# Sixteen gate products, placed between the parts of the recurrence batches instead of behind the last batch

## The chip, the cores and the metric

The kernel runs on one core of a Trainium2 chip. The metric is the device time of the program in microseconds (us). Three runs of the kernel before took 3376.48, 3397.38 and 3405.18 us; the median is 3397.38 us. One further execution was profiled.

## The reference, cut to what matters

The program computes two transformer-like blocks. The change lies in the first one, in its token mixer, where a Hyena branch and an RWKV-7 branch are joined by gates:

```python
def token_mixer(h, p, states0):
    cols = h @ p['w_in']
    hy_cols, rw_cols, gate_cols = jnp.split(cols, (HY_COLS, HY_COLS + RW_COLS), axis=-1)
    y_hy = hyena_branch(hy_cols, p) @ p['hy_proj']
    y_rw, finals = rwkv_branch(rw_cols, p, states0)
    g_hy, g_rw = jnp.split(jax.nn.sigmoid(gate_cols), 2, axis=-1)
    mixed = (g_hy * y_hy + g_rw * (y_rw @ p['rw_proj'])) @ p['w_out']
    return mixed, finals
```

There are 512 tokens of width 1024, and 256 context tokens that only give start states. The RWKV recurrence `S <- S (diag(w) + a^T b) + v^T k` runs over the tokens for 8 heads of 64 and in both directions. The gates need `h` and `w_in` alone: they depend on no recurrence, and nothing in the recurrences depends on them.

## The kernel before, in words

**The recurrences.** `rwkv` (line 627) cuts them into six batches. Batches 0 and 1 are the context, batches 2 to 5 the 512 tokens, one pair of heads in both directions each. Time is cut into chunks of 64, inside which the recurrence becomes matrix products and one triangular inverse. A batch has these parts:

- `rw_start`: the products of h with w_in for k, v and r (`win_mm`, 24 matmuls of 128x512 each, tiles `mm<-hTh,wh`), the norm of k (lines 723, 732, 738; its end is `kk`, L769), the low-rank products (L797), then a run of DVE, ACT and POOL steps (L799 to L833) that ends with `kms` (L840).
- `rw_gram`: products of one chunk with itself (L863), in four pieces, masked on ACT and DVE.
- `rw_inverse`: DVE alone. L891 transposes, then 31 pairs of L899 and L900, the substitution row by row.
- `rw_blocks`: L910 and L911 on DVE, then two sets of 32x32 products (L920, L928), copied by ACT (L923, L931).
- `rw_rows` and `rw_ops`: transposes and products (L953 to L993, then L1020, L1033).
- `rw_chain`: the states in order, each step two small matmuls (L1063) and one DVE operation (L1068), and then the output `py` (L1081, L1084), copied out by ACT (L1086).
- `rw_end`: the group norm of the output (L704 to L715); that of the last batch ends with L712.

In the loop (line 662) the start and gram of batch i+1 are written ahead of the inverse, blocks, rows and chain of batch i. The tile `AR` has two buffers, so the start of batch i+2 cannot finish writing it before the `py` of batch i has read it.

**The gates.** `fill` (line 548) makes 16 gates, one for each 128 columns: eight of kind `wgh`, eight of kind `wgr`. For each, `h_mm` (line 262) loads two halves of the weight (tag `wf`, four buffers that the loaded, the high and the low part share), makes the high part on ACT (L279) and the low part on POOL (L280), and issues 24 matmuls in float32r (L285 to L287, tiles `sm<-hTh,wh`; `sm` has one buffer). ACT takes the tanh (L556), POOL scales it (L557), multiplies it for `wgh` (L561) and writes it to memory (L562). In the code all of it stands behind the last batch.

**What sets the order.** The tile framework orders each engine's instructions when the program is built. The text order is the priority; work that stands later in the text is moved up where the scheduler's own model finds an engine free. So some of the gates stood inside the batches already. On the chip each engine then takes its instructions in that fixed order.

**What follows.** `mix_out` (line 1260) closes the pools of the recurrences, loads the outputs of the batches (L1282), multiplies them by their gate (L1283), and multiplies by `rw_proj` (L1292 for the first three batches, L1300 for the last).

Of the kernel before, what the change touches and what calls it, by code (L numbers as in the profile page):

```python
# [178 lines left out]
class K:  # L179
# [365 lines left out]
            nc.scalar.activation(o, ps, AF.Copy)  # L545
            nc.gpsimd.dma_start(self.mhd[c], o)

    def fill(self, pool):

        nc, I = self.nc, self.I  # L550
        for w_, dst in (("wgh", self.mhd), ("wgr", self.grd)):
            for c in range(KD):
                ps = self.psum("sm", 1)
                self.h_mm(ps, I[w_][c], "wf", self.nwf, nc.gpsimd)
                g = self.rw["wk"].tile([P, T], F32, name="hyo")
                nc.scalar.activation(g, ps, AF.Tanh, scale=0.5)  # L556
                nc.gpsimd.tensor_scalar(g, g, 0.5, 0.5, op0=OP.mult, op1=OP.add)  # L557
                if w_ == "wgh":
                    h = self.rw["wk"].tile([P, T], F32, name="hyi")
                    nc.gpsimd.dma_start(h, self.mhd[c])  # L560
                    nc.gpsimd.tensor_tensor(g, g, h, op=OP.mult)  # L561
                nc.gpsimd.dma_start(dst[c], g)  # L562

    def skip(self, moe):

        xp = self.xp = self.pool(self.top, "xp", side="right")
        self.X = xp.tile([P, TT, D], F32, name="X")
        self.nc.sync.dma_start(self.X, self.I["t_x"])
        with ExitStack() as es:
            z = self.pool(es, "zp").tile([P, 512], F32, name="zz")  # L570
            for t in range(TT if not moe else 0):
                for h in range(2):
                    self.nc.vector.memset(z, 0.0)
                    self.add_to_x(t, h, z)
        self.open_stream(6)
        with ExitStack() as es:
            w1 = self.pool(es, "w1")
            self.silu_vec(w1)
            self.mtag = "tr"
            for g in (1, 2) if moe else ():  # L580
                list(self.lat_group(g, w1))
            list(self.ada_group(0, 0, w1))
            if not moe:
                for g in range(3):
                    list(self.ada_group(1, g, w1))
                list(self.s5_prep(w1))
        if moe:
            self.mes = ExitStack()
            self.rtw = self.pool(self.mes, "yl").tile([P, KD, NEXP], F32, name="rtw")
            self.nc.sync.dma_start(self.rtw, self.I["rtw"])  # L590
            self.open_moe()
            self.route_weights()
            with ExitStack() as es:
                wk = self.pool(es, "mo2", bufs=2)
                for t in range(TT):
                    self.route_logits(t, wk, *self.route_tile(t, wk, wk.tile([P, KD, P], F32, name="h2T"), wk.tile([P, D], F32, name="junk")))
                for t in range(TT):
                    self.first_rows(t)
                self.first_rank(0, wk)
# [27 lines left out]
    def rwkv(self):  # L627


        nc, I = self.nc, self.I  # L630
        V, G = nc.vector, nc.gpsimd
        es = ExitStack()
        self.nwi, self.wit = 4, "wi"
        with es:
            cst = self.pool(es, "rwc")
            wk = self.pool(es, "rwk")
            wupa = cst.tile([P, 2, 512], F32, name="wupa")
            nc.scalar.dma_start(wupa[0:64], I["wup"])
            nc.scalar.dma_start(wupa[64:128], I["aup"])
            mid = cst.tile([P, 14], F32, name="mumid")  # L640
            mu0, mu1 = self.col("rw_mu", 0, 14), self.col("rw_mu", 14, 14)
            V.tensor_tensor(mid, mu0, mu1, op=OP.add)
            V.tensor_scalar(mid, mid, -1.0, 1.0, op0=OP.mult, op1=OP.add)
            h = cst.tile([P, 2, 8], F32, name="halfb")
            V.tensor_scalar(h[:, 0], self.col("rw_w0", 0, 8), 0.5, None, op0=OP.mult)
            V.tensor_scalar(h[:, 1], self.col("rw_a0", 0, 8), 0.5, None, op0=OP.mult)
            ka = cst.tile([P, 2, 4], F32, name="ka")
            V.tensor_scalar(ka[:, 0], self.col("rw_k_a", 0, 4), 0.5, None, op0=OP.mult)
            V.tensor_scalar(ka[:, 1], self.col("rw_k_a", 0, 4), -0.5, 1.0, op0=OP.mult, op1=OP.add)

            S0 = cst.tile([P, 8, CH], F32, name="S0")
            LLc = cst.tile([P, TC], F32, name="LLc")
            LL = cst.tile([P, T], F32, name="LL")
            self.rw = dict(wupa=wupa, halfb=h, ka=ka, S0=S0, wk=wk, mid=mid)
            self.mix(12, self.win_mm(24, True), LLc)
            self.mix(12, self.win_mm(24), LL)
            nc.scalar.activation(LLc[0:64], LLc[0:64], AF.Tanh)
            nc.scalar.activation(LL[0:64], LL[0:64], AF.Tanh)
            B = [dict(cts=(2 * i, 2 * i + 1), n=TC, LL=LLc) for i in range(2)] + [dict(cts=(i,), n=T, LL=LL) for i in range(4)]
            self.rw_start(B[0])  # L660
            self.rw_gram(B[0])
            for i, b in enumerate(B):
                if i + 1 < len(B):
                    self.rw_start(B[i + 1])
                    self.rw_gram(B[i + 1])
                self.rw_inverse(b)
                self.rw_blocks(b)
                self.rw_rows(b)
                self.rw_chain(b)
                if b["out"]:  # L670
                    self.rw_end(b)
                if i == 0:
                    self.hy_out()
                    self.rw_gate()
            self.fill(None)
            self.dump("d_S0", S0)

    def mix(self, i, ps, out):
# [1758 lines left out]
```

## Time and profile before

| | |
|---|---|
| median of three runs | 3397.38 us |
| profiled execution | 3396.03 us, span 3394.3 us |
| PE (TensorE matmul) busy over the span | 92% |
| DVE, ACT, POOL busy | 48%, 28%, 21% |
| mean granted TensorE clock | 0.947 |

The recurrences of the tokens lie between about 404 and 846 us, the rest of the gates between 846 and 896 us. A busy PE in this profile is not PE at its peak: matmuls overlap, and their ends are modelled. "Idle before" is time in which an engine had nothing running, with what ended it. An instruction that fails to find its input holds up all that is behind it on the same engine.

### The profile page before, as it was taken

How to read it: one execution, taken by the hardware profiler on the slowest of the kernel's cores; microseconds unless marked ns; L12 is line 12 of the kernel's file. 1: busy time of each engine (PE TensorE's matmuls, PEld its weight loads, DVE VectorE, ACT ScalarE, POOL GpSimd, SP SyncE). 2: the span in 40 equal slices, each digit the busy share in tenths (PEclk: the TensorE clock that was granted, in tenths of full speed). 3: DMA queues.
4: the chain of work that ended last, by engine and by line, in shares of the span. 5: the costliest groups of instructions: out<-in, count | busy, mean ns of one | idle time of the engine just before them, and what ended most of it. 6: DMA issues, size and time to landing. Idle time of an engine off the chain costs nothing.

```text
span 3394.3 us, 42711 instructions
## 1 busy us (share of the span) xinstructions
PE 3128.7 (92%) x16973; PEld 1973.0 (58%) x16973; DVE 1627.2 (48%) x2862; ACT 942.7 (28%) x1707; POOL 729.3 (21%) x793
## 2 busy tenths in 40 slices
PE   8989989989789999999999988899888998999999
PEld 3646556666465334333333257565776777778887
DVE  3665887663052211110110146775676776546464
ACT  3313443332131111111101032246331332234242
POOL 1031231333320143330000033110596002210000
PEclk9998997869989999999999999789998998999999
DMA  5643210001559999999999954310336465422221
GB/s 217 222 175 106 66 38 29 29 32 57 211 198 356 372 421 420 420 421 421 420 421 421 420 219 160 124 56 13 121 127 220 158 203 153 140 81 97 96 99 69
DMA packets 144591, 681.41 MB, mean 201 GB/s; under 512 B 25455, under 2 KB 33815, under 8 KB 76424
## 3 DMA queue, kind: packets, MB, share of 16 engines
q1 hardware_dynamic: 134480, 652.44, 50.4%
q0 software_dynamic: 5536, 18.16, 1.4%
q10 hardware_dynamic: 4376, 8.09, 0.7%
q8 instruction: 134, 2.20, 0.3%
q14 instruction: 65, 0.53, 0.0%
HBM read 654.50 MB, written 24.12 MB: 200 GB/s over the span
## 4 chain that ended last, share of the span: by engine, by line
PE 56%; DMA 17%; DVE 12%; POOL 8%; issue 4%; ACT 3%; SPq 0%; ACTq 0%; POOLq 0%; DVEq 0%
DMA we<-in_w_dram 13%; PE mm L1635 8%; PE mm L285 5%; PE mm L286 5%; PE mm L287 5%; PE ch L1667 3%; POOL cug L2051 3%; PE sm L287 2%; PE sm L286 2%; PE sm L285 2%; PE tr L1549 2%; DMA wa<-in_adaw_dram 2%; POOL sca L2052 1%; DVE macc L347 1%; PE sm L1598 1%
## 5 line engine op out<-in xcount | busy, mean ns | idle before, releaser
L1635 PE MATMUL mm<-we,XG 128*64 128x512 f32 x2048 | 473.4, 601 | 4.2 <-DMA we<-in_w_dram 3.4
L285 PE MATMUL mm<-hh,wh 128*128 128x512 f32 x704 | 281.3, 400 | 22.8 <-DVE vg L2005 18.5
L1635 PEld LDWEIGHTS mm<-we,XG 128*64 128x64 f32 x2048 | 134.1, 137 | 273.2 <-issue 254.1
L286 PE MATMUL mm<-hl,wh 128*128 128x512 f32 x704 | 277.6, 394 | 0.0
L1667 PE MATMUL ch<-we,hid 128*64 128x512 f32 x1024 | 263.2, 598 | 13.0 <-DMA we<-in_w_dram 12.9
L287 PE MATMUL mm<-hh,wl 128*128 128x512 f32 x704 | 271.8, 394 | 0.0
L1590 DVE SCALAR_TENSOR_TENSOR hth<-hth,tr 128x256 f32<-128x256 f32 x64 | 27.0, 421 | 394.3 <-ACT hth L1589 393.8
L1667 PEld LDWEIGHTS ch<-we,hid 128*64 128x64 f32 x1024 | 94.8, 136 | 170.4 <-issue 132.2
L285 PEld LDWEIGHTS mm<-hh,wh 128*128 128x128 f32 x704 | 134.1, 190 | 65.3 <-issue 25.9
L347 DVE SCALAR_TENSOR_TENSOR macc<-wa,cvs,macc 128x512 f32<-128x512 f32 (+1 forms) x119 | 151.6, 1291 | 34.1 <-DMA wa<-in_adaw_dram 29.5
L470 POOL TENSOR_TENSOR X<-X,gy 128x512 f32<-128x512 f32 x20 | 28.2, 1433 | 591.5 <-DVE gy L1737 591.5
L280 DVE TENSOR_TENSOR wl<-wu,wh 128x1024 fp32r<-128x1024 f32 x88 | 118.1, 1343 | 72.4 <-ACT wh L279 72.1
L287 PEld LDWEIGHTS mm<-hh,wl 128*128 128x128 f32 x704 | 134.0, 190 | 29.3
L286 PEld LDWEIGHTS mm<-hl,wh 128*128 128x128 f32 x704 | 134.4, 191 | 26.9 <-POOL hl L464 0.6
L1603 DVE TENSOR_TENSOR acc<-acc,sm 128x512 f32<-128x512 f32 x48 | 33.0, 687 | 236.4 <-PE sm L1598 236.4
L1646 ACT ACTIVATE hs<-mm 128x512 f32<-128x512 f32 x64 | 38.2, 597 | 386.9 <-PE mm L1635 380.2
L279 ACT ACTIVATE wh<-wu 128x1024 fp32r<-128x1024 f32 x88 | 93.3, 1060 | 132.6 <-PE mm L286 99.9
L280 DVE TENSOR_TENSOR wl<-wd,wh 128x1024 fp32r<-128x1024 f32 (+1 forms) x48 | 56.9, 1187 | 95.4 <-ACT wh L279 95.4
L1720 POOL TENSOR_TENSOR ess<-ess,mhalf 128x1 f32<-128x1 f32 x4 | 3.2, 792 | 442.7 <-DVE ess L1719 442.6
L279 ACT ACTIVATE wh<-wd 128x1024 fp32r<-128x1024 f32 (+1 forms) x48 | 47.5, 989 | 166.9 <-PE sm L287 78.6
L285 PE MATMUL mm<-hTh,wh 128*128 128x512 f32 x208 | 88.0, 423 | 6.1 <-ACT th L799 4.1
L287 PE MATMUL mm<-hTh,wl 128*128 128x512 f32 x208 | 86.8, 418 | 5.9 <-DVE wl L280 5.9
(835 smaller groups left out, 6683.8 us busy)
## 6 DMA issues: line engine op xcount, KB each, us to landing
we<-in_w_dram SPq DMA_DIRECT2D x384, 1024.0 KB, 14.7
wu<-in_wupf_dram SPq DMA_DIRECT2D x44, 1024.0 KB, 4.8
wa<-in_adaw_dram SPq DMA_DIRECT2D x24, 1024.0 KB, 5.1
wa<-in_adaw_dram SPq DMA_DIRECT2D x96, 256.0 KB, 4.8
wa<-in_modw_dram SPq DMA_DIRECT2D x16, 1024.0 KB, 7.0
wd<-in_wdn_dram SPq DMA_DIRECT2D x16, 1024.0 KB, 4.8
aw<-in_awin_dram SPq DMA_DIRECT2D x12, 1024.0 KB, 5.2
wi<-in_win_dram SPq DMA_DIRECT2D x46, 256.0 KB, 2.6
```

The lines of the kernel that those rows point to most:

```text
L279: self.nc.scalar.activation(h, x, AF.Copy)
L280: (E or self.nc.vector).tensor_tensor(l, x, h.bitcast(F32), op=OP.subtract)
L285: mm(ps, a[0], b[0], start=start, stop=False)
L286: mm(ps, a[0], b[1], start=False, stop=False)
L287: mm(ps, a[1], b[0], start=False, stop=stop)
L347: V.scalar_tensor_tensor(a, w, c, a, op0=OP.mult, op1=OP.add)
L1549: nc.tensor.matmul(ps[:, c * i:c * i + c], self.xn[:, t, o:o + P], oh[:, t], start=(t == 0), stop=(t == TT - 1), skip_group_check=True)
L1598: nc.tensor.matmul(pc, G[:, P * t:P * t + P], ye[:, 512 * n:512 * n + 512], start=True, stop=True)
L1635: mm = nc.tensor.matmul(ps[64 * h:64 * h + 64], XG[:, k, CAP * e:CAP * e + CAP], w[:, i, h], start=(k == 0), stop=(k == KD - 1), skip_grou ...
L1646: nc.scalar.activation(hs, ps, AF.Copy)
L1667: mm = nc.tensor.matmul(py[n][64 * h:64 * h + 64], hid[h][:, f], ww[h][:, i, 512 * n:512 * n + 512], start=(f == 0), stop=(f == 15), skip_ ...
L2051: E.tensor_tensor(u[k], p[k][1], p[k][0], op=OP.mult)
```

## The change

`fill` becomes a generator that stops behind each gate. The loop takes one gate at three places of every batch from the second on: between the start and the gram of the next batch, behind that gram, and behind the inverse. Batch 5 has no next batch, so it takes two. Two gates are left over and stay behind the loop. No instruction is added or taken away, and the buffers are the same.

```diff
--- before.py
+++ after.py
@@ -545,7 +545,7 @@
             nc.scalar.activation(o, ps, AF.Copy)
             nc.gpsimd.dma_start(self.mhd[c], o)
 
-    def fill(self, pool):
+    def fill(self):
 
         nc, I = self.nc, self.I
         for w_, dst in (("wgh", self.mhd), ("wgr", self.grd)):
@@ -560,6 +560,7 @@
                     nc.gpsimd.dma_start(h, self.mhd[c])
                     nc.gpsimd.tensor_tensor(g, g, h, op=OP.mult)
                 nc.gpsimd.dma_start(dst[c], g)
+                yield
 
     def skip(self, moe):
 
@@ -659,11 +660,18 @@
             B = [dict(cts=(2 * i, 2 * i + 1), n=TC, LL=LLc) for i in range(2)] + [dict(cts=(i,), n=T, LL=LL) for i in range(4)]
             self.rw_start(B[0])
             self.rw_gram(B[0])
+            gates = self.fill()
             for i, b in enumerate(B):
                 if i + 1 < len(B):
                     self.rw_start(B[i + 1])
+                    if i:
+                        next(gates)
                     self.rw_gram(B[i + 1])
+                if i:
+                    next(gates)
                 self.rw_inverse(b)
+                if i:
+                    next(gates)
                 self.rw_blocks(b)
                 self.rw_rows(b)
                 self.rw_chain(b)
@@ -672,7 +680,8 @@
                 if i == 0:
                     self.hy_out()
                     self.rw_gate()
-            self.fill(None)
+            for _ in gates:
+                pass
             self.dump("d_S0", S0)
 
     def mix(self, i, ps, out):
```

Line numbers below line 663 grow by 1 to 9: L863 is L872 in the changed kernel, L928 is L937, L1292 is L1301.

**PE, from the end of the gram of batch 3 to the rows of batch 2.** `tr<-AR,BK` is the gram, `ch<-X,GA` and `ch<-TTt,FT` are the two sets of block products, `ch<-misc,zv` is the first of the rows; `mm` with `hTh` or `hTl` is a product of a later start, `sm` with them is a gate. Before:

```order
L863 MATMUL tr<-AR,BK 128x128 x8
L920 MATMUL ch<-X_3390,GA 32x32 x32
L287 MATMUL mm<-hTh,wl 128x512
L285 MATMUL mm<-hTh,wh 128x512
L863 MATMUL tr<-AR,BK 128x128 x4
L286 MATMUL mm<-hTl,wh 128x512
L287 MATMUL mm<-hTh,wl 128x512
L928 MATMUL ch<-TTt,FT 32x32 x32
L953 MATMUL ch<-misc,zv 128x128 x2
```

and now:

```order
L872 MATMUL tr<-AR,BK 128x128 x4
L286 MATMUL sm<-hTl,wh 128x512
L287 MATMUL sm<-hTh,wl 128x512
L285 MATMUL sm<-hTh,wh 128x512
L286 MATMUL sm<-hTl,wh 128x512
L287 MATMUL sm<-hTh,wl 128x512
L937 MATMUL ch<-TTt,FT 32x32 x16
L285 MATMUL sm<-hTh,wh 128x512
L286 MATMUL sm<-hTl,wh 128x512
L287 MATMUL sm<-hTh,wl 128x512
L285 MATMUL sm<-hTh,wh 128x512
```

The gates now stand between the gram and the rows. Behind these rows ten more gate matmuls come, one block product, ten gate matmuls, fifteen block products, and then the rows: 29 gate matmuls from the gram to the first L1020, where there was one.

**ACT, in the start of batch 4.** `th`, `ta`, `kms` and `km` belong to the start, `FT` and `TTt` to the blocks of batch 3, `UV` and `AG` to its rows, `yr` and `ysq` to the end of batch 2. Before:

```order
L799 ACTIVATE ta<-mm,halfb 128x512
L707 ACTIVATE ysq<-yr 128x512
L923 ACTIVATE FT<-ch 32x512 x2
L931 ACTIVATE TTt<-ch 32x16x32 x2
L815 ACTIVATE kms<-ta,ka 128x512
L957 ACTIVATE UV<-ch 64x2x128
L958 ACTIVATE UV<-ch 64x2x128
L957 ACTIVATE UV<-ch 64x2x128
L958 ACTIVATE UV<-ch 64x2x128
L966 ACTIVATE AG<-ch 128x8x64
L799 ACTIVATE th<-mm,halfb 128x512
L799 ACTIVATE ta<-mm,halfb 128x512
```

and now:

```order
L808 ACTIVATE th<-mm,halfb 128x512
L810 ACTIVATE th<-th 128x512
L808 ACTIVATE ta<-mm,halfb 128x512
L817 ACTIVATE PC<-th 128x8
L824 ACTIVATE kms<-ta,ka 128x512
L818 ACTIVATE th<-E 128x512
L819 ACTIVATE E<-E 128x520
L808 ACTIVATE th<-mm,halfb 128x512
L808 ACTIVATE ta<-mm,halfb 128x512
L810 ACTIVATE th<-th 128x512
L824 ACTIVATE km<-ta,ka 128x512
L556 ACTIVATE hyo<-sm 128x512
```

The copies for the blocks and the rows of batch 3 no longer stand inside the start of batch 4.

**PE, at the end of the recurrences.** `pp` is the last batch's output and its norm, `tr<-xn,rwp` the first product of `mix_out`. Before, with 158 gate matmuls between the last norm and L1408, behind which L1292 starts:

```order
L704 MATMUL pp<-yr,misc 128x512
L287 MATMUL sm<-hTh,wl 128x512
L285 MATMUL sm<-hTh,wh 128x512
L286 MATMUL sm<-hTl,wh 128x512
L287 MATMUL sm<-hTh,wl 128x512
L723 MATMUL pp<-misc,ysq 128x2 x4
L285 MATMUL sm<-hTh,wh 128x512
L286 MATMUL sm<-hTl,wh 128x512
```

and now:

```order
L1090 MATMUL pp<-AR,SP 64x64 x2
L1093 MATMUL pp<-GR,UV 64x64 x2
L713 MATMUL pp<-yr,misc 128x512
L732 MATMUL pp<-misc,ysq 128x2 x4
L741 MATMUL pp<-misc,rny 8x128
L1301 MATMUL tr<-xn_6755,rwp 128x512
L747 MATMUL pp<-rty,misc 64x128 x8
L1301 MATMUL tr<-xn_6755,rwp 128x512 x3
L1301 MATMUL sm<-xn_6755,rwp 128x512 x3
```

No gate matmul stands behind the last output any more, and the products of `mix_out` follow at once. Counted in PE's order, from the last product of `rw_gate` (L693) to the end of the gram of batch 2, from there to the end of the next gram and so on, the gate matmuls were 11, 34, 24, 40 and, behind the gram of batch 5, 275. They are now 43, 72, 73, 67 and 129. From the end of each of the four grams (batches 2 to 5) to the next L1020 there were 0, 1, 0 and 5 gate matmuls and 24, 80, 24 and 43 of the rows (as PE's order counts them); now there are 29, 29, 28 and 41, and 80, 80, 80 and 76.

## Rows read from the trace of the kernel before

**Rows 1.** Busy time by stretch: us, then PE, PEld, DVE, ACT, POOL, clock, DMA share, GB/s.

```profile
404.00:457.90 53.90, 47.05 (x433) 33.33 (x431) 36.26 (x57) 29.88 (x60) 19.78 (x21) 1.00 0.18 59
457.90:532.10 74.20, 64.38 (x576) 45.39 (x576) 64.67 (x130) 29.70 (x60) 25.03 (x23) 0.90 0.13 40
532.10:634.80 102.70, 96.19 (x983) 68.48 (x981) 61.62 (x132) 42.27 (x89) 26.41 (x26) 0.77 0.08 27
634.80:734.70 99.90, 90.10 (x844) 63.69 (x846) 67.06 (x132) 34.68 (x72) 34.31 (x33) 0.77 0.10 33
734.70:846.10 111.40, 102.03 (x1316) 72.05 (x1313) 50.90 (x117) 31.51 (x66) 33.98 (x37) 0.93 0.16 51
846.10:895.80 49.70, 40.41 (x153) 27.62 (x151) 0.04 (x1) 11.73 (x19) 22.32 (x24) 0.97 0.36 121
```

**Rows 2.** Groups of instructions of 846.2 to 895.8 us: busy, mean ns | idle before.

```profile
L287 PE MATMUL sm<-hTh,wl 128*128 128x512 f32 x51 | 21.6, 423 | 4.5 <-POOL wl L280 4.5
L280 POOL TENSOR_TENSOR wl<-wf,wh 128x512 fp32r<-128x512 f32 x12 | 15.2, 1268 | 23.3 <-PE sm L286 19.5 <-ACT wh L279 2.6 <-PE sm L287 1.2
L556 ACT ACTIVATE hyo<-sm 128x512 f32<-128x512 f32 x7 | 4.2, 597 | 8.2 <-PE sm L287 8.1
```

**Rows 3.** Instructions in order of time, end of the recurrences: start, us, what [idle before].

```profile
845.45 0.69 DVE L712 TENSOR_TENSOR yl<-yr,kms 128x512 f32<-128x512 f32 x1
...
903.93 0.17 DVE L1409 COPY br<-sm 128x16 f32<-128x16 f32 x1 [57.79 <-DMA grd<-hyo]
...
905.88 1.19 PE L1292 MATMUL sm<-xn,rwp 128*128 128x512 f32 x1 [8.03 <-DVE xn L1283]
```

**Rows 4.** Chain of waits, 400 to 850 us: start us, us, what.

```profile
531.30 1.04 PE ch L953 x4
...
549.75 1.20 DVE MT L1024 x2
```

**Rows 5.** DVE in order of time: lines 769, 840 and 910 of batches 3 to 5.

```profile
492.58 0.68 DVE L769 TENSOR_TENSOR kk<-kk,mm 128x512 f32<-128x512 f32 x1
514.90 0.68 DVE L840 TENSOR_TENSOR kms<-tr,zv 128x512 f32<-128x512 f32 x1
577.87 0.69 DVE L769 TENSOR_TENSOR kk<-kk,mm 128x512 f32<-128x512 f32 x1 [1.17 <-PE mm L738]
623.81 0.68 DVE L840 TENSOR_TENSOR kms<-tr,zv 128x512 f32<-128x512 f32 x1
683.56 0.67 DVE L769 TENSOR_TENSOR kk<-kk,mm 128x512 f32<-128x512 f32 x1
692.82 2.20 DVE L910 STREAM_TRANSPOSE X<-Xi 128x1024 f32<-128x1024 f32 x1
716.63 0.69 DVE L840 TENSOR_TENSOR kms<-tr,zv 128x512 f32<-128x512 f32 x1 [2.17 <-PE tr L839]
774.22 2.05 DVE L910 STREAM_TRANSPOSE X<-Xi 128x1024 f32<-128x1024 f32 x1
```

**Rows 6.** ACT in order of time: outputs of batches 2 to 4, and batch 3's blocks.

```profile
592.18 0.60 ACT L1086 ACTIVATE yr<-pp 128x512 f32<-128x512 f32 x1 [7.49 <-PE pp L1084]
608.27 1.19 ACT L931 ACTIVATE TTt<-ch 32x512 f32<-32x512 f32 x2 [5.00 <-PE ch L928]
613.88 0.69 ACT L799 ACTIVATE th<-mm,halfb 128x512 f32<-128x512 f32 x1 [1.38 <-POOL BK L820]
675.52 0.60 ACT L1086 ACTIVATE yr<-pp 128x512 f32<-128x512 f32 x1 [12.42 <-PE pp L1084]
779.68 0.60 ACT L1086 ACTIVATE yr<-pp 128x512 f32<-128x512 f32 x1 [6.25 <-PE pp L1084]
```

**Rows 7.** Busy time of three stretches at the lower clock, columns as in Rows 1.

```profile
568.80:613.20 44.40, 43.98 (x343) 28.51 (x344) 17.11 (x32) 10.52 (x19) 15.51 (x18) 0.50 0.07 25
681.40:701.90 20.50, 18.66 (x146) 10.39 (x146) 14.65 (x21) 6.73 (x12) 9.90 (x10) 0.50 0.07 26
708.70:736.00 27.30, 23.88 (x132) 19.74 (x132) 12.44 (x18) 11.96 (x30) 9.27 (x7) 0.50 0.05 15
```


## The prediction

> **What bounds the kernel now.** I read the table of busy time by stretch first. Its inner edges are the starts of line 891, with which the inverses of batches 2 to 5 open [rows 1]. While the recurrences run, every stretch has PE busy for 87 to 94% and DVE for 46 to 87%, at a mean clock between 0.77 and 1.00. From 846.1 to 895.8 us DVE does nothing: PE works on gates alone, 153 matmuls in 49.7 us, 0.325 us each, and is idle for 9.3 us of that. The second view, the groups of that tail, shows for what: it waits 4.5 us for the low parts that POOL makes, and the rest is the wait for ACT to empty the one `sm` buffer, since ACT itself waits for the last matmul of each gate [rows 2]. Third, the instructions in order of time at its end: the last DVE step of the recurrences ends at 846.1 us, and the first product of `mix_out` starts at 905.9; DVE was idle for 57.8 us and was released by the last gate's write [rows 3]. These 59.7 us are what the change can save. Fourth, the DVE and ACT steps inside the batches show what a later PE would push [rows 5, 6].
>
> **What the change saves.** In the new order no gate matmul stands behind the last output, and the loads for `mix_out` and its first products stand ahead of L712's release. I take the whole 59.7 us, in which the last write and the closing of the pools are included (846.1 to 905.9) [rows 3]. The products may even start some us ahead of L712; I leave that uncounted, since the loads of `wo` and `X` still wait for the pools.
>
> **What it costs.** No instruction is added: 146 gate matmuls (275 less 129 behind the gram of batch 5) go into the four stretches ahead. What matters is where they queue. From the end of a gram to the first L1020 PE's order held 0, 1, 0 and 5 gate matmuls; it now holds 29, 29, 28 and 41, 121 more. A gate matmul at the tail's price is 0.325 us, stalls included [rows 1]. In two of these places 56 and in one 33 products of the rows come behind the gram too, which used to be mixed into the start before it. For these I have the stretch from the first L953 to L1024 of batch 2, 18.4 us for 80 of them with what stands between [rows 4], or 0.23 us each. Behind both wait the chain and the output of that batch, and the start of the batch after next, which needs that output read.
>
> - Stretch 457.9 to 532.1: 29 x 0.325 + 56 x 0.23 = 22.3 us later for the chain of batch 1, and so for `kk` of batch 3 (492.6 us) [rows 5]. What leaves the start of batch 2 shortens the stretch before, and twelve fewer products stand here; I take 12.
> - Stretch 532.1 to 634.8: 28 x 0.325 = 9.1 us later for the output of batch 2 (592.2 us) [rows 6]. Before, the start of batch 4 took 45.9 us from `kk` to `kms`, where that of batch 3 took 22.3 [rows 5]: ACT came to its second half only at 613.9 us, right behind the copies for the blocks of batch 3 [rows 6]. These stand behind the gram now. But `kk`, which came 14 us ahead of the output, now comes behind it, some 8 us if it goes as with batch 5 (675.5 to 683.6) [rows 5, 6]. So `kms` comes 8 + 22.3 = 30.3 us behind the output, against 31.6 before. I take 6, rounded down since the lower clock of this place [rows 7] may end sooner.
> - Stretch 634.8 to 734.7: 28 x 0.325 + 56 x 0.23 = 22.0 us later for the output of batch 3 (675.5 us). The start of batch 5 took 33.1 us because the inverse of batch 4 kept DVE until 692.8 [rows 5, 6]. With `kk` 22 us later the inverse is over, the start takes 22.3, and `kms` comes at 727.9 in place of 716.6: 11.
> - Stretch 734.7 to 846.1: 36 x 0.325 + 33 x 0.23 = 19.3 us later for the output of batch 4, which came 5.5 us behind the end of the inverse of batch 5 (779.7 against 774.2) [rows 5, 6], so little is slack; part of the blocks of batch 5 stands ahead of that output now. I take 13.
>
> POOL makes twelve more low parts inside the stretches (1.27 us each [rows 2]). It was busy for 25 to 34% of them [rows 1], and I cost them at nothing; if that cover fails, it is through the steps that a start needs of POOL. SP and DMA I also cost at nothing: they were busy for 8 to 16% [rows 1].
>
> **Sum.** 59.7 - (12 + 6 + 11 + 13) = 18 us saved. The profiled execution took 3396.0 us (span 3394.3 and 1.7 around it), so 3378; the median of the runs is 1.4 above it, and I forecast **3379 us**. The ends of the cost are nothing (all 121 matmuls lie in waits that are there anyway: 60 us saved, 3337) and the four full sums, 22.3 + 9.1 + 22.0 + 19.3 = 72.7 (13 us lost, 3410). A second way comes near it: 146 matmuls at the tail's busy time (40.41 us for 153 [rows 1], 0.264 each) are 39 us more on the 400 that PE is busy from 404 to 846.1; at the same busy share of 90% these stretches would grow by 43 us, against the 42 above.
>
> How full PE is decides between these ends. By the busy time, the five stretches leave it 42 us idle in all [rows 1], fewer than 146 x 0.325 = 47; but the weight loads were busy for only 283 of the same 442 us. The Trainium skill, in "Perfetto Trace Analysis", section "Identifying the Most-Contended Engine", says that busy matmul time is a poor measure of how near TensorE is to its limit, and that the busy share of weight loads should be read. By that rule there are 159 us of room, the moved matmuls would all fit, and the sum would be the 3337 of the first rival. The trace bears it out in part: where nothing waits, the matmuls overlap. It does not say that the room lies where the moved matmuls queue.
>
> **Rivals.**
> - *All covered* (20%). The moved matmuls lie in the latency of starts and blocks, and the granted clock rises with them. For it: three stretches of 92 us together ran at the lower level, 1.2 GHz, with small products and waits, and PE was busy for 86.5 us of them [rows 7]. Every 10 us of these that go back to 2.4 GHz give up to 5. Against it: the counts above, which put most of the matmuls in front of rows that are ready. 60 us saved, 3337; with a clock that is higher as well, some 3325. The Trainium skill ("TensorE: Matmul & The Clock Gate", section "HAM oscillation — how this bites in real kernels") holds that waits between bursts of matmuls bring the clock down; the first of these stretches agrees in its small products, but not in idle time, which is 0.4 us.
> - *All in series* (28%): the one that ends slower. The gates in front of the rows delay every output by their full price, and no start gets shorter. It decides from 59.7 us of cost on: that is 82% of the 72.7. For it: the blocks of batch b were ready before the gram of b+1 ended (L910 at 692.8, gram's end at 734.7) [rows 1, 5], so PE could have gone on. 13 us lost, 3410. Where a stretch has the lower clock, a matmul costs up to twice as much: a third of it so (0.77 to 0.93 of the mean clock [rows 1]) adds up to 24 us, 3434.
> - *The end does not move as far* (7%). The tail also hid loads for `mix_out` (a DMA share of 0.36 against 0.08 to 0.16 before it [rows 1]). Some 12 us of them come to light: 3391.
>
> **How the numbers follow.** The forecast has 45%, with 15 us to either side, which no row bounds more closely. The range 3333 to 3414 leaves out the far ends of the first two rivals. About 1% (34 us) is what a measurement of this kernel can tell from no change; its runs lie 29 us apart. Faster by more than that, under 3363: nearly all of the first rival and a tenth of the forecast, and a little for an error in the saving, 0.27. Slower, over 3431: a quarter of the second rival, 0.07. Within: 0.66.
>
> **What would show it.** In the new profile L1301 (was L1292) should start within 5 us of the end of L721 (was L712); if it starts over 10 us later, the saving was wrong. The starts of L900 (was L891) should lie 70 to 90, 100 to 115 and 105 to 118 us apart, against 74.2, 102.7 and 99.9. If they are no further apart than before, the first rival is right; if the last batch ends over 905 us, the second. The second half of the start of batch 4 should no longer wait for the copies of blocks. The forecast is wrong above all if POOL or the single `sm` buffer stops PE longer inside the batches than in the tail.

## The result, and the profile after

The change took 3407.81 us (median of 20 runs, 3391.27 to 3418.56), the kernel before 3383.93 us on the same chip (20 runs, 3376.03 to 3405.18). The ratio is 1.0058, with a 95% interval of 1.0042 to 1.0073: slower by some 20 us, where I forecast 18 us less. A second comparison gave 1.0038 (1.0026 to 1.0050). The profiled execution of the change took 3399.3 us, with a span of 3397.5.

I read the table by stretch first, as in [rows 1]; its inner edges are the starts of line 900 (was 891), and the last one is the end of line 721 (was 712).

```profile
404.00:463.40 59.40, 53.27 (x271) 37.49 (x272) 33.88 (x45) 23.54 (x45) 26.40 (x25) 0.82 0.20 62
463.40:552.10 88.70, 81.51 (x708) 56.40 (x707) 66.39 (x127) 38.78 (x78) 33.40 (x36) 0.89 0.18 55
552.10:670.20 118.10, 105.15 (x934) 73.40 (x934) 72.18 (x134) 39.53 (x80) 40.78 (x39) 0.82 0.14 43
670.20:786.80 116.60, 103.20 (x991) 72.39 (x991) 70.73 (x133) 41.09 (x84) 33.82 (x34) 0.79 0.10 33
786.80:917.60 130.80, 116.61 (x1398) 83.77 (x1398) 54.67 (x120) 36.04 (x75) 27.85 (x32) 0.85 0.24 80
```

The four stretches from the inverse of batch 2 on took 74.2, 102.7, 99.9 and 111.4 us; they now take 14.5, 15.4, 16.7 and 19.4 more. The one ahead of them, from the inverse of batch 1 to that of batch 2, grew from 88.9 to 97.6. Together that is 74.7 us. (In a second trace of the kernel before, that first one took 95.8 us, with the gram of batch 2 at the lower clock, so most of its growth is within what one execution differs from the next.)

The end, in order of time (start, us, what), answers to [rows 3]:

```profile
911.80 1.91 PE L1301 MATMUL tr<-xn,rwp 128*128 128x512 f32 x2
...
917.04 0.69 DVE L721 TENSOR_TENSOR yl<-yr,kms 128x512 f32<-128x512 f32 x1
917.82 0.17 DVE L1418 COPY br<-sm 128x16 f32<-128x16 f32 x1
```

The mix starts 5.9 us ahead of the end of L721, so the gates behind the last batch are gone as forecast. But it starts at 911.8 where it started at 905.9: the loop gives up more than the end gained. In the rest of the program the two traces run alike (2485.7 us from there to the end, 2488.4 before).

The DVE steps of a start and the outputs on ACT answer to [rows 5, 6]:

```profile
444.35 0.68 DVE L849 TENSOR_TENSOR kms<-tr,zv 128x512 f32<-128x512 f32 x1
...
541.18 0.68 DVE L849 TENSOR_TENSOR kms<-tr,zv 128x512 f32<-128x512 f32 x1
...
627.56 0.68 DVE L778 TENSOR_TENSOR kk<-kk,mm 128x512 f32<-128x512 f32 x1
650.25 0.68 DVE L849 TENSOR_TENSOR kms<-tr,zv 128x512 f32<-128x512 f32 x1
735.42 0.67 DVE L778 TENSOR_TENSOR kk<-kk,mm 128x512 f32<-128x512 f32 x1
765.78 0.69 DVE L849 TENSOR_TENSOR kms<-tr,zv 128x512 f32<-128x512 f32 x1 [0.36 <-PE tr L848]
```

```profile
615.33 0.60 ACT L1095 ACTIVATE yr<-pp 128x512 f32<-128x512 f32 x1 [8.39 <-PE pp L1093]
731.88 0.60 ACT L1095 ACTIVATE yr<-pp 128x512 f32<-128x512 f32 x1 [13.76 <-PE pp L1093]
846.21 0.60 ACT L1095 ACTIVATE yr<-pp 128x512 f32<-128x512 f32 x1 [6.41 <-PE pp L1093]
```

From `kk` to `kms` batch 4 now takes 22.7 us (45.9 before), as I had said. What ate it stands behind `kms`: until L900 there it is 20.0 us (650.2 to 670.2), where it was 11.0 [rows 1, 5]. PE in order of time shows with what:

```profile
643.14 0.39 PE L286 MATMUL sm<-hTl,wh 128*128 128x512 f32 x1
643.38 0.39 PE L287 MATMUL sm<-hTh,wl 128*128 128x512 f32 x1
...
647.51 2.07 PE L848 MATMUL tr<-kms,misc 128*128 128x512 f32 x2 [2.61 <-DVE kms L846]
649.51 2.07 PE L872 MATMUL tr<-AR,BK 64*128 64x128 f32 x8
651.51 0.79 PE L287 MATMUL sm<-hTh,wl 128*128 128x512 f32 x1
652.11 0.63 PE L285 MATMUL sm<-hTh,wh 128*128 128x512 f32 x1
652.53 0.63 PE L286 MATMUL sm<-hTl,wh 128*128 128x512 f32 x1
653.09 3.09 PE L872 MATMUL tr<-AR,BK 64*128 64x128 f32 x16
...
668.89 0.79 PE L287 MATMUL sm<-hTh,wl 128*128 128x512 f32 x1
669.49 0.63 PE L285 MATMUL sm<-hTh,wh 128*128 128x512 f32 x1
```

From L848 on no row has an idle time: PE works through, with three gate matmuls between any two pieces of the gram, twelve in all. The busy time of that stretch, columns as in [rows 1]:

```profile
647.40:674.70 27.30, 27.19 (x121) 20.10 (x122) 12.79 (x24) 6.41 (x15) 11.47 (x12) 0.50 0.13 39
```

The granted clock is at its lower level, 1.2 GHz. One gate matmul follows the other there after 0.42 us (652.11 to 652.53), at 643 us, at the higher level, after 0.24. The inverse waits for all of this gram.

Are the twelve matmuls or the clock to blame? The gram of batch 3 in the same trace has twelve gate matmuls between its pieces too, and from `kms` to L900 it took 10.9 us, at the higher level:

```profile
541.15 0.39 PE L285 MATMUL sm<-hTh,wh 128*128 128x512 f32 x1
541.91 1.71 PE L872 MATMUL tr<-AR,BK 64*128 64x128 f32 x16 [0.37 <-DVE kms L849]
543.55 0.50 PE L286 MATMUL sm<-hTl,wh 128*128 128x512 f32 x1
```

```profile
541.20:552.10 10.90, 10.44 (x72) 7.83 (x70) 5.60 (x14) 4.58 (x12) 3.87 (x5) 1.00 0.19 54
```

In a second trace of the change the same gram took 18.1 us at a clock of 0.50, and in a second trace of the kernel before the gram of batch 2, without any gate, took 17.0 us at 0.50 where it had taken 11.0 at 1.00. So in a gram the clock costs 6 to 7 us. Against the rows' and the next start's products that stood there before, the twelve matmuls cost nothing that shows at the higher level, and some 2 to 3 us at the lower (19.0 against 17.0 for batch 2, 21.0 against 18.1 for batch 5). Why the clock falls in one gram and not in another, no run here shows.

The POOL rows of the same start show a second queue:

```profile
639.47 1.27 POOL L280 TENSOR_TENSOR wl<-wf,wh 128x512 fp32r<-128x512 f32 x1 [1.47 <-PE sm L286]
640.70 2.21 POOL L825 TENSOR_TENSOR km<-km,zk 128x512 f32<-128x512 f32 x1
642.88 1.05 POOL L557 TENSOR_SCALAR hyo<-hyo 128x512 f32<-128x512 f32 x1
643.91 1.77 POOL L842 TENSOR_TENSOR kms<-kms,km 128x512 f32<-128x512 f32 x1
```

A gate's low part (`wl`) and a gate's scaling stand ahead of `km` and `kms`, for which PE waits 2.61 us at L848.

### The profile page after: what moved, and what is told of

Read it like the earlier page. It is cut to its first block, busy times and chain, and to the rows that moved or that the text cites. A ratio compares the mean times of both kernels' runs of the same rounds, so it can differ in the third digit from the quotient of the medians.

```text
span 3397.5 us, 42699 instructions
## 1 busy us (share of the span) xinstructions
PE 3144.0 (93%) x16973; PEld 1983.4 (58%) x16973; DVE 1646.3 (48%) x2862; ACT 941.3 (28%) x1707; POOL 725.6 (21%) x793
## 4 chain that ended last, share of the span: by engine, by line
PE 57%; DMA 15%; DVE 13%; POOL 8%; issue 4%; ACT 2%; SPq 0%; ACTq 0%; POOLq 0%; DVEq 0%
DMA we<-in_w_dram 13%; PE mm L1644 9%; PE mm L285 5%; PE mm L286 5%; PE mm L287 5%; PE ch L1676 3%; POOL cug L2060 3%; PE sm L286 2%; PE sm L287 2%; PE sm L285 2%; PE tr L872 2%; PE tr L1558 2%; DVE Xt L908 2%; DVE Xi L909 2%; POOL sca L2061 1%
```

## The experiments

Three theories: (1) the loop has no room, and every gate costs there what it adds; (2) count: there is room for about eight gates, wherever they stand, and no more; (3) place: a gate costs by what it stands in front of. In the results, **loop** is the time from L891 of batch 0 to the end of the last L704 (PE's first product over the last batch's output), and **end** from there to the first product of the mix, L1292. The kernel before has 519.3 and 69.3 us, the change 592.5 and 5.6. The planner had moved nine of the sixteen gates of the kernel before into the loop.

**No gate in the loop** (`tail_all`). This kernel puts all sixteen gates behind the last batch. A block under `pinned` may not be ordered ahead of PE's last instruction in front of it.

```diff
-                    if i:
-                        next(gates)
...
-            for _ in gates:
-                pass
+            with self.pinned(EP.PE):
+                for _ in gates:
+                    pass
```

> All sixteen gates stand behind the last batch: TensorE may not start one before its last instruction of the recurrences; no gate is left in the loop. Theory 1, the loop has no room for gates (each costs there what it adds in the change, 75 us of longer stretches over 8 more gates = 9.4 us, at any place and for the first eight too): the stretches of the loop shorten by about 8 x 9.4 = 75 us against the kernel before, the end behind the last batch grows by 8 x 7.5 = 60 us to about 120 us, the whole is 3384 - 15 = about 3369 us. Theory 2, the loop has room for about eight gates and the change overfills it (the first eight beside waits, mostly in the last two chains of steps, the next eight in series): the loop shortens by 25 us or less, the whole is 3384 + 35 = about 3419 us or more.

It took 3468.67 us, ratio 1.0228 (1.0174 to 1.0283): loop 521.4, end 148.8 us. The loop is no shorter without gates, so the nine of the kernel before had cost it nothing: theory 1 falls, theory 2 is right on this. Why they are free shows in the last batch. Busy time from the products just ahead of its steps to the end of the loop, columns as in [rows 1], in the kernel before and then without gates:

```profile
805.60:836.60 31.00, 29.83 (x360) 19.67 (x356) 7.71 (x20) 3.13 (x6) 7.01 (x7) 1.00 0.15 49
```

```profile
805.10:835.50 30.40, 23.73 (x314) 15.92 (x310) 7.56 (x20) 0.70 (x2) 0.00 (x0) 0.61 0.00 1
```

The same instructions in 31.0 us with some 46 matmuls more, in 30.4 without: each step waits for DVE, and the gates stand in those waits. Two steps of the kernel before in order of time on PE, and two without gates:

```profile
815.70 0.33 PE L1063 MATMUL ch<-SP,MT 64*64 64x64 f32 x4
815.96 0.51 PE L287 MATMUL sm<-hTh,wl 128*128 128x512 f32 x1
816.30 0.40 PE L285 MATMUL sm<-hTh,wh 128*128 128x512 f32 x1
816.54 0.40 PE L286 MATMUL sm<-hTl,wh 128*128 128x512 f32 x1
816.87 0.33 PE L1063 MATMUL ch<-SP,MT 64*64 64x64 f32 x4
```

```profile
815.08 0.48 PE L1067 MATMUL ch<-SP,MT 64*64 64x64 f32 x4 [0.39 <-DVE SP L1072]
815.95 0.48 PE L1067 MATMUL ch<-SP,MT 64*64 64x64 f32 x4 [0.39 <-DVE SP L1072]
```

A step with three gate matmuls is 1.17 us long, without them 0.87, so the waits don't hide all of them. What the steps lose, the output behind them gets back: its pairs of products (L1081 and L1084) follow each other after 0.53 us with gates and 0.82 without, since the clock over this stretch is 1.00 with them and 0.61 without. Over the whole loop, again before and without gates, it is 0.87 and 0.76:

```profile
317.30:836.60 519.30, 470.87 (x4794) 327.76 (x4792) 351.84 (x726) 203.06 (x417) 155.48 (x159) 0.87 0.13 42
```

```profile
314.10:835.50 521.40, 449.94 (x4577) 312.96 (x4576) 337.61 (x726) 188.63 (x392) 109.38 (x109) 0.76 0.08 25
```

**Eight gates at one place, eight behind** (`two_start`, `two_gram`, `two_chain`). As the kernel above, with two gates in each of the four rounds that start one of the batches 2 to 5:

```diff
                     self.rw_start(B[i + 1])
+                    for _ in range(2 if i and i + 1 < len(B) else 0):
+                        next(gates)
                     self.rw_gram(B[i + 1])
```

In the second kernel the loop with `next` stands behind `rw_gram`, in the third behind `rw_chain`. The inverse has no instruction of PE's, so a piece ahead of it and one behind it have the same place in PE's order.

> Eight gates in the loop, two each between start and gram of the batches 2 to 5, and eight behind the last batch, where TensorE may not start them earlier: the count of the kernel before in the loop, but at the first of the three places alone. Theory 1 (a gate costs the same at any place of the loop): within 6 us of the kernel before, 3378 to 3390 us. Theory 3, the place decides (gates beside the start's chain over VectorE and ScalarE are covered, those behind the gram stand in TensorE's queue ahead of rows that are ready): 10 to 25 us below the kernel before, 3360 to 3374 us, and 20 us or more below the kernel with two behind the gram.

> As the kernel with two gates between start and gram, but with the two behind the gram of the next batch, ahead of the inverse. Theory 1: within 6 us of the kernel before and of that one, 3378 to 3390 us. Theory 3: the rows of the running batch wait behind 24 to 48 gate matmuls more, 10 to 25 us above the kernel before, 3394 to 3409 us.

> As these two, but with the two gates behind the steps of the running batch, ahead of its end: those that the planner moves up can stand between steps that wait for VectorE. Theory 1: 3378 to 3390 us. Theory 3: the steps' waits hide gates, but the next start's products stand there already and are pushed back; 3370 to 3384 us. If the two kernels with other places and this one lie within 6 us of each other, the place doesn't decide.

| | us | ratio (95%) | loop | end |
|---|---|---|---|---|
| two_start | 3404.13 | 1.0049 (1.0028 to 1.0070) | 535.1 | 82.2 |
| two_gram | 3437.04 | 1.0144 (1.0103 to 1.0185) | 550.4 | 80.6 |
| two_chain | 3414.70 | 1.0076 (1.0045 to 1.0108) | 537.6 | 81.1 |

At the same count the loops of `two_start` and `two_gram` differ by 15 us and their ratios lie apart, so the place counts; `two_start` and `two_chain` can't be told apart. No written place is as good as the nine free ones of the planner. All three are slower than either theory's range. I had expected `two_start` to be faster than the kernel before, and it was not: its eight gates add 14 us to the loop without gates, where the planner's nine add none.

**Sixteen at the start** (`four_start`), with 4 in place of 2 in the diff above.

> All sixteen gates in the loop, as in the change, but all of them at one of its three places: four each between start and gram of the batches 2 to 5, none ahead of the inverse or of the blocks, none behind the last batch. Theory 2 (count: the loop has room for about eight gates, whose cost was nothing in the kernel before against none at all, and the next eight cost 70 us wherever they stand): the last batch's sum over its output (L712 of the change) ends near 905 us of the span and the whole is near the change, 3400 to 3415 us. Theory 3 (place: eight gates at this place put that end at 847 us, eight behind the gram at 868 us): 1.4 to 3 us a gate, the end at 860 to 885 us, the whole 3360 to 3385 us.

3389.81 us, ratio 0.9987 (0.9968 to 1.0005), in neither theory's range. The loop took 590.6 us, like that of the change: for its length, count decides (theory 2), and the best of the three places doesn't cover sixteen. But 33 of the mix's 64 products (L1298 here) stand in this loop too, from 805.5 us on, between the products and the steps of the last two batches, where this kernel has no gate:

```profile
880.73 0.33 PE L1069 MATMUL ch<-SP,MT 64*64 64x64 f32 x4
880.99 1.12 PE L1298 MATMUL tr<-xn,rwp 128*128 128x512 f32 x2
882.04 0.33 PE L1069 MATMUL ch<-SP,MT 64*64 64x64 f32 x4
```

So its **end** can't be compared. A mark that can is the end of the mix's last product: from L891 of batch 0 to there it took 613.0 us, the change 631.1, the kernel before 618.3. The 18 us less agree with the medians of the runs, which lie 18 us apart; behind this mark its trace is 6 us longer than that of the change. So for the whole time the count doesn't decide alone: it also matters what stands between the last steps.

**Two at the start, the rest where the planner finds room** (`two_start_free`): the same 2, but the remaining eight without `pinned`.

> Two gates each between start and gram of the batches 2 to 5, as in the kernel with two at the start, but the other eight are traced behind the last batch without a bond, so that the planner moves four of them up between the steps of the last two batches, where TensorE waits for VectorE; 89 gate matmuls stay behind the end. Theory 2: the twelve gates cost some 35 us of the loop and save 33 us of the end: 3380 to 3395 us. Theory 3: the four between the last steps are hidden as those of the kernel before were; the end of the loop stays at 847 us and the part behind it falls from 82 to about 45 us: 3360 to 3372 us.

3377.25 us, ratio **0.9935** (0.9911 to 0.9959), between the two ranges, and the first that is clearly faster than the kernel before: loop 531.1, end 44.6. Four gates more than `two_start` in the loop, and the loop 4 us shorter. They stand between the steps of the last two batches, where no start's products compete for PE. That they make it shorter isn't shown: up to the inverse of batch 5 the two kernels have nearly the same order on PE and their traces differ by 10 us (428.1 and 417.8), the gram of batch 3 alone by 6, at clocks of 0.50 and 1.00. So of the 14 us that `two_start` adds, some 10 may belong to its one execution. From the inverse of batch 5 to the end of the loop it is 113.3 us with the four and 106.9 without. The last batch again:

```profile
817.60:847.40 29.80, 28.71 (x357) 19.18 (x354) 7.68 (x20) 3.80 (x7) 6.18 (x7) 1.00 0.16 52
```

**Three at the start** (`three_start_free`), the other four free.

> Three gates each between start and gram of the batches 2 to 5 (twelve), the last four traced behind the last batch without a bond; the planner moves all four up into the steps of the last two batches, none stays behind the end. With two each the end of the loop was 847 us at twelve gates in all, with four each 910 us at sixteen. If the start's room ends at two a batch: four gates more at 8 to 9 us each, the end at 880 to 885 us, no gates behind it, the whole equal to the kernel with two each within 6 us: 3371 to 3383 us. If the steps of the last two batches are the room and three a batch still cost 1.5 us a gate: the end at 853 us and the whole 3345 to 3358 us.

3372.96 us, ratio 0.9944 (0.9922 to 0.9966): loop 569.1, end 8.0. The first branch of the expectation: four gates more at the start cost 38 us, 9.5 each, and save 36.6 at the end. All 38 lie between `kms` and the inverses (92.3 us in the four batches, 53.7 in `two_start_free`). So with four free between the last steps, the start takes two a round cheaply and no third.

**The change without its first place** (`no_start`): nine gates at the other two, the count in the loop as in `two_start_free`.

```diff
                     self.rw_start(B[i + 1])
-                    if i:
-                        next(gates)
                     self.rw_gram(B[i + 1])
```

> The change without the first of its three places: one gate behind each gram and one behind each inverse (nine in all), none between start and gram; the rest traced behind the last batch, where the planner moves some up between the last steps and leaves 86 gate matmuls behind the end, as in the kernel with two at the start and the rest free (89). So the same count in the loop and behind it, at the other two places. If the count decides: within 6 us of that kernel, 3371 to 3383 us, the end of the loop near 847 us. If the place decides (eight behind the gram put the end 21 us later than eight at the start): the end near 866 to 875 us, the whole 3394 to 3405 us.

3391.37 us, ratio 1.0008 (0.9987 to 1.0029), a little under the second range: loop 551.8, end 44.3. With the same twelve in the loop, 20.7 us more than at the start: theory 3, at this count. Of these, 19.2 lie between `kms` and the inverses (72.9 us against 53.7), and the clock differs there: 0.50 or 0.51 in all four, against 0.91 to 1.00. How much of it is the place by itself isn't separated. On PE this kernel has the order of `two_gram` up to the inverse of batch 5, with four more gates between the last steps: loop 551.8 against 550.4, end 44.3 against 80.6. That is the cleaner sign that those four are all but free.

**What of a gate costs** (`thin16`, `nopool16`). The change, first with one gate product in three (the gates come out coarser), then with the low parts off POOL: ACT copies the weights, and the subtraction is left out.

```diff
+                if thin:
+                    self.nc.tensor.matmul(ps, (l if k == 1 or k == 5 else h)[:, o], self.hT[0][:, k], start=k == 0, stop=k == KD - 1)
+                    continue
```

```diff
+        if E is self.nc.gpsimd and self.in_rwkv:
+            self.nc.scalar.activation(l, x, AF.Copy)
+            return
```

> The change with a third of the gates' TensorE work: of the three products that make one gate matmul, one is left (8 matmuls a gate for 24), so the gates' values are coarser; weights, their high and low parts, tanh and stores all stay. The planner moves some of the shorter pieces, but none is behind the last batch. If TensorE's time on the gates is what lengthens the change's loop (71 us over a loop without gates): the last batch's sum ends at 835 to 850 us in place of 906 and the whole is 3330 to 3350 us. If it is what feeds them (loads on SP's queue, high parts on ScalarE, low parts in GpSimd's queue ahead of the start's products): the end stays at 880 us or later and the whole at 3380 us or more.

> The change with the gates' low parts made by ScalarE, as a plain copy of the weights (the subtraction is left out), so GpSimd does no split in the recurrences; TensorE's order stays nearly the same. In the change's chain of waits GpSimd's low parts stand ahead of the start's products km and kms. If they cost time there (1.27 us each, 1 to 3 in each of four starts): the end of the loop 5 to 15 us earlier than 906 us, the whole 3393 to 3403 us. If TensorE's order alone decides: 906 us within 4, the whole within 5 us of the change, 3403 to 3413 us.

`thin16` took 3330.6 us, ratio 0.9835 (0.9796 to 0.9874): loop 534.4. Of the 73 us that the change adds to the loop, 58 go with two thirds of the gates' matmuls; loads, high and low parts, tanh and stores were all still there. The planner also put the shorter pieces elsewhere, and 33 of the mix's products into this loop, so part of the 58 may be place. The whole loop, columns as before, for this kernel and then for the change:

```profile
314.30:848.70 534.40, 489.70 (x4754) 337.24 (x4754) 366.00 (x730) 215.19 (x438) 185.52 (x187) 0.82 0.17 58
```

```profile
313.80:906.30 592.50, 534.87 (x4977) 371.41 (x4976) 372.10 (x729) 215.89 (x438) 181.35 (x187) 0.85 0.17 53
```

PE is busy for 92% of the one and 90% of the other: the busy share doesn't tell that 256 matmuls are gone. `nopool16` took 3386.81 us, 1.0008 (0.9985 to 1.0030): loop 581.4. So POOL's low parts were worth 11 us of the loop, which I had costed at nothing; 7 of them lie in the starts of batches 4 and 5, from the output of the batch before last to `kms`.

**The end of the kernel before alone** (`tail_fast`).

```diff
-                ps = self.psum("sm", 1)
-                self.h_mm(ps, I[w_][c], "wf", self.nwf, nc.gpsimd)
+                last = w_ == "wgr"
+                ps = self.psum("mm", 2) if last else self.psum("sm", 1)
+                self.h_mm(ps, I[w_][c], "wf", self.nwf, nc.vector if last else nc.gpsimd)
```

> The kernel before with its end alone changed: the second eight gates, nearly all of which stand behind the last batch, take turns on two PSUM buffers in place of one, and the low part of their weights is made by VectorE, which idles there, not by GpSimd. The 59.8 us from the last batch's sum to the mix held 42.4 us of TensorE work and 17.4 us of its waits, most of them for GpSimd's low part and for the one PSUM buffer. If those waits set the end: 10 to 16 us less, 3368 to 3378 us. If the weights' loads set it (9.1 MB in that stretch at 153 GB/s): within 4 us of the kernel before.

3388.56 us, ratio 0.9992 (0.9976 to 1.0008): no gain that can be told. PE's waits between the gates did go; the groups of 846 to 900 us, against [rows 2]:

```profile
L287 PE MATMUL mm<-hTh,wl 128*128 128x512 f32 x50 | 21.4, 428 | 0.3 <-DVE wl L280 0.2
L285 PE MATMUL mm<-hTh,wh 128*128 128x512 f32 x50 | 21.2, 424 | 0.9 <-ACT wh L279 0.4
...
L1293 PE MATMUL sm<-xn,rwp 128*128 128x512 f32 x1 | 1.2, 1193 | 11.0 <-DVE xn L1284 11.0
```

The wait for the low part fell from 4.5 us to 0.2, and the end from 69.3 to 63.8, not by the 10 to 16 I expected: 11.0 us of PE's waiting stand at the mix itself, for the loaded gates. That the loads of weights held the rest was not tested by itself.

**Both kernels once more** (`before_again`, `after_again`), for second traces.

> The kernel before once more, for a second trace. Its first took 519.3 us from the second batch's start to the last sum, 69.3 us from there to the mix, 2488.4 us behind it. If the loop is the same work in every run: 519 within 3 us, 69 within 3 us, and what differs between runs lies behind the mix (2475 to 2490 us). If the first trace of before was a long one of its kind: the loop or the end is 8 us or more shorter.

> The change once more, for a second trace. Its first took 592.5 us from the second batch's start to the last sum, 5.6 us to the mix, 2485.7 us behind it. If the missing 14 to 17 us lie in the loop: 600 us or more there. If they lie in the spread behind the mix: 592 within 4 us, and the rest longer than that of the kernel before by 8 us or more, or within the spread of 2473 to 2490 us that the ten traces so far show for the same instructions.

Loop, end and the rest were 522.7, 69.2 and 2493.1 us, and 595.1, 5.6 and 2485.8. So the loop costs 72 to 73 us and the end gives 64 in both pairs, and neither trace of the change has the 8 us more in the loop. Each pair of traces stands 3 us apart at its end, the timed runs 13 to 24. The end of the mix's last product shows more of it: from L891 of batch 0 to there the change took 631.1 and 633.7 us, the kernel before 618.3 and 622.0, so 12 to 13 us more in both pairs. Behind it the traces of the change are 6 and 10 us shorter (2453 us twice, 2459 and 2463 before); over all the traces that part took 2444 to 2463 us. The runs list a mean clock of 0.94 for the change and 0.946 for before (medians of 10 and 19 runs of this comparison); the two traced executions of before had 0.947 and 0.942 and took 3396 and 3401 us, above the median of its runs. So some 12 us of the loss have a place in the program; where the runs that were not traced gain the rest stays open.

## Why the prediction was wrong

**The saving was right.** I took 59.7 us, with the mix within 5 us of the end of L712. It starts 5.9 us ahead of it, so the end gave 65.6 us by this mark, 64 by the one of the experiments. My base was 13 us high: 3397.38 us from three runs, where the median of twenty is 3383.93. That 3407.81 lies inside my range owes something to this.

**The cost was the step that failed: 12 + 6 + 11 + 13 = 42 us, where the traces show 73 to 75.** I took 30.7 us off the four full sums for gains in return, and had no term for the grams. The path through the loop, cut at the marks that the rows show (us, for the first pair of traces; the second pair gives 60.5, 15.7, -4.7 and 0.9):

| pieces | before | change | more |
|---|---|---|---|
| behind a gram: L891 of batch 2 to `kms` of batch 3, L891 of b+1 to the output of b for b = 2, 3, 4 | 202.8 | 262.1 | 59.3 |
| gram: `kms` to L891, batches 2 to 5 | 57.3 | 71.0 | 13.7 |
| start: output of batch 2 to `kms` of 4, of 3 to 5 | 72.7 | 68.8 | -3.9 |
| the rest: L891 of batch 0 to `kms` of 2, output of 4 to the end | 186.5 | 190.6 | 4.1 |

The rival *All in series* (72.7, no start shorter) is what happened, and its sign came: the last batch ended at 917.7 us, over 905. That its sum meets the 73.2 is chance: behind the grams it was 59.3, and the grams came on top.

- *Behind the grams the delay was real, and nearly all of it is the gates.* The four pieces grew by 20.8, 3.1, 21.0 and 14.4 us, for which the full sums were 22.3, 9.1, 22.0 and 19.3. Nearly half of these sums I had given to the rows that moved. In `thin16` most of these rows stand behind the grams too, with at most four gate matmuls between a gram and L1020, and the same four pieces took 203.3 us, as in the kernel before. So no cost of the rows shows, and a gate matmul cost more than my 0.325 us: if all 59.3 us are the 121's, 0.49 each.
- *The gains in return didn't come.* That the start of batch 4 would no longer wait for the copies of blocks was right (22.7 us from `kk` to `kms`). But its `kms` comes 34.9 us behind the output of batch 2, 31.6 before, where I had 30.3. For the start of batch 5 I had said 22.3, and it took 30.4 (33.1 before). Together the two starts gave back 3.9 us. The output of batch 4, and with it the last batch, has moved by 66.5 us by then (779.7 to 846.2).
- *The grams had no term.* I had counted the matmuls behind a gram, and left out those between its pieces, as if the start's latency hid them. From `kms` to the inverse batch 2 took 11.0 us before and 19.0 now, batch 4 11.0 and 20.0, batch 5 18.1 and 21.0; only batch 3 got shorter, 17.2 and 10.9. By the rows above most of this is the clock, which was at its lower level in one gram and a part of another before, and in three now; some 2 to 3 us a gram are the matmuls at that level. This is the larger part of the 8.7 us in the stretch ahead of batch 2's inverse, and of the 15.4 in the third, over its full sum of 9.1.
- *POOL at nothing was wrong*, in the way I had named: 11 us by `nopool16`, the larger part of them in the starts that were to get shorter.
- *The room.* From idle time I had 42 us of it, and from the share of weight loads 159. Nine gates cost nothing and the next seven 73 us, 10.5 each. The Trainium skill ("Perfetto Trace Analysis", section "Identifying the Most-Contended Engine") holds that the weight loads' share tells more than busy time. The runs agree as far as a busy share of 86 to 92% in every loop, with or without gates, said nothing of the room; they also show that the nine had taken what could be had between the last steps, so the average, 60 to 65% in weight loads, didn't say it either.

The first rival, *All covered*, is refuted for the gates that were moved; for the nine that the planner had moved before it is true. The third, that loads of the mix would come to light, didn't show: the mix started ahead of L721.

## What to carry to other kernels

A planner that has moved half of a filler into the gaps has taken the free half: before the other half is forced in, take the first out and see whether the loop gets shorter. Only the two kernels that placed a part of the gates by hand and left the rest to the planner were faster than the one before (0.9935 and 0.9944). Price a forced piece where it is queued, each of its places for itself, at the clock of that place, and count the queue of every engine that feeds it. Two traces of one kernel can have different clocks in the same place (10.9 and 18.1 us here for the same gram), so look at more than one before a few us are put down to an edit. Filler belongs between dependent steps with nothing else to do (here the last two batches' states), not in front of rows on which the next output hangs.

## What was not expected of the hardware

Work in the gaps paid for itself through the clock. The last batch's steps and output ran at a mean granted clock of 0.61 without gates and 1.00 with three gate matmuls in a gap, and took about as long (31.0 us with them, 30.4 without). In the change the same gates ran in places where PE had no wait at all and the clock was still at its lower level: 27.2 us busy of the 27.3 from 647.4 to 674.7 us, at 0.50.
